# Six places of the instruction order in a decoder-step kernel: where the convolution state is loaded, where squares, one projection step and the last outputs stand, and which order edges there are

## The chip, the cores and the metric

The kernel runs on one core of a Trainium2 chip as one program. The metric is the device time in microseconds (us) of one execution. The five engines appear as PE (TensorE), DVE (VectorE), ACT (ScalarE), POOL (GpSimd) and SP (SyncE, which issues the DMA transfers). Each engine runs its instructions in the order in which the program lists them and waits on semaphores for the others.

## The reference

One layer of a hybrid decoder for 2048 prompt tokens, and for 8 sample sequences of 4 new tokens each. Model width is 1024, the FFN is 2816 wide, all in fp32. Cut to what matters:

```python
def mixer(xn, s0, lp):
    q, k, v, r, a, u, sv = split_cols(xn @ w_in)
    logg = log_sigmoid(a @ w_alpha + b_alpha) / GLA_TAU
    o, S = gla_chunked(q, k, v, logg, s0)          # gated linear attention, with a state
    o = rmsnorm(o, g_gla_out) * silu(r)
    z = sgu_spatial(rmsnorm(gelu(sv), g_sgu), w_s, b_s)
    return concatenate([o, gelu(u) * z], -1) @ w_out, S, sv

def mem_kv(mem, g_mem, wk_x, wv_x):                # 256 memory tokens
    mn = rmsnorm(mem, g_mem)
    return mn @ wk_x, mn @ wv_x

def conv_ffn(hn, buf, w_gate, w_up, conv_w, conv_b, w_down):
    gp = concatenate([buf, hn @ w_gate], axis=1)   # buf: the last two rows (state_conv)
    c = conv_b + sum(conv_w[j] * gp[:, j:j + T] for j in range(3))
    return (gelu(c) * (hn @ w_up)) @ w_down, gp[:, -2:]

h = x + mixer(rmsnorm(x, g_mix), s0, ...)
h = h + mem_attend(rmsnorm(h, g_x), mk, mv, wq_x, wo_x)
h = h + conv_ffn(rmsnorm(h, g_ffn), buf, ...)      # and a final rmsnorm
```

## The kernel before

**Tiling.** The prompt is worked in four sub-blocks of 512 tokens, s = 0 to 3. The 32 sample tokens ride along in the mixer of sub-block 1 (544 columns, as two chunks of 272) and in the FFN of sub-block 2. "Mixer 0" and "mixer 1" are here the mixers of s = 0 and s = 1. Activations lie with the features on the 128 partitions. Every fp32 product is three matmuls of rounded parts (`mm3`, lines 97 to 101): high x high, high x low, low x high. For that, each weight tile is loaded raw (`r_...`, at most 5 in flight), ScalarE writes the rounded part (`h_...`, L84) and VectorE the rest (`l_...`, L85). PSUM has four banks for accumulators (`acc`) and four for everything else (`mps`).

**What sets the order.** The program is a list of `Step`s. `weave(main, (steps, first, last), ...)` spreads side steps over the positions first to last of a main list, and `run` goes through the list and loads weights 5 units ahead. A scheduler of the framework then puts the instructions of each engine in order by a time simulation of its own. `behind(first, then)` adds an edge that only says that `then` comes later in the order than `first`; it makes no semaphore wait between engines.

**Startup.** `mem_load` loads the memory tokens into four buffers `mx`, which the first x tiles `x0` use after them. `mem_norm` transposes them (`mtp`), multiplies by the gain and splits (`mh`, `ml`), and squares them on ScalarE (`junk<-mx`, summed per row in `mss`). The inverse norm is spread to all partitions (`mbc`, copied to `mbcs`). `mem_proj` makes k and v of one head at a time: 48 matmuls `mkp`/`mvp` into two accumulators, which VectorE empties with a multiplication by `mbcs` into `mkf`. `mem_turn` transposes the result for the output (`mkt`, `mvt`), one head later. `late_constants` loads small constants, and the convolution state `state_conv` as six tiles `sc0` to `sc5` with 22 small transposes into one bank `sctp`, copied to `sct`. The FFN of sub-block 2 is the first to read `sct`.

**Mixer 0** also folds weights of the memory attention (`qk_steps`, `vo_steps`): a vo step multiplies two 128-row parts `vr` of v with a weight `wof` (12 matmuls `vop`, two evictions `voh`, `vol`). Of the linear attention, `s0pl` are score matmuls of head pair p and level l, whose inputs `e` and `kr` VectorE and ScalarE make one level after the other. `decay` makes `kh` (VectorE, ScalarE, then POOL), which `keys_turned` transposes (`ktp`). `t_wr` are the gate's projections, `zp` the spatial products, `op` the attention outputs, whose normed and gated form `o` is transposed back as `otp`.

**Output projection.** `out_proj_steps` gives w1, half the sum over the upper inputs (`ch4` to `ch7`, tiles `wo s 4 m`), and w2, the half over the lower ones (`ch0` to `ch3`, from `otp`). Only `whole` sub-blocks (0, 2, 3) keep both halves in one accumulator. In mixer 1 all four w1 steps (`wo140` to `wo143`, 48 matmuls of 272 columns each) stand ahead of the four of w2 (`wo100` to `wo103`), and the edge behind `B.last_o` in `half` does apply to whole sub-blocks only, because it asks for `not end`. After w2 come the memory scores (`sc10...`), which need h of all eight row tiles and sums of them (`wog`, `w1wo`, `wulwo` and others).

**Tail.** `last_rows` makes the last row tiles of y: the product `dr` added to `ht`, squares on ScalarE, a reciprocal root by VectorE and POOL (`rstd_of`, tiles `rt`, `yss`), and the outputs `y`. The outputs of row c follow the norm of row c + 1.

Of the kernel before, what the change touches and what calls it, by code (L numbers as in the profile page):

```python
# [37 lines left out]
def hymba_step_kernel(  # L38
# [48 lines left out]
    def split_scaled(hi, lo, src, g):  # L87
        act.activation(hi, src, AF.Copy, scale=g)
# [223 lines left out]
    def rstd_of(out, ss, p, n, inv):  # L312
        t = narrow("rt")
        dve.tensor_scalar(t[:p, :n], ss, inv, EPS, ALU.mult, ALU.add)
        pool.tensor_tensor(out, t[:p, :n], neghalf[:p, :n], ALU.pow)

# [139 lines left out]


# [76 lines left out]
    def mem_norm():  # L534
        xt, ss = mem_st.xt, narrow("mss")
        mem_st.pair = []
        for k2 in range(4):
            ps = mps(f"mtp{k2}")
            for kk in range(2):
                k = 2 * k2 + kk  # L540
                for c in range(2):
                    pe.transpose(ps[:, kk * 256 + c * 128:kk * 256 + (c + 1) * 128],
                                 xt[c][k // 4][:, (k % 4) * 128:(k % 4 + 1) * 128], ident)
            hi, lo = U(f"mh{k2}", F32R), U(f"ml{k2}", F32R)
            for kk in range(2):
                s = slice(kk * 256, (kk + 1) * 256)
                split_scaled(hi[:, s], lo[:, s], ps[:, s], gcol("gmem", 2 * k2 + kk))
                mem_st.pair.append((hi[:, s], lo[:, s]))
        for c in range(2):
            for j in range(2):  # L550
                act.activation(junk, xt[c][j][:, :512], AF.Square, accum_out=ss[:, 2 * j + c:2 * j + c + 1])
# [9 lines left out]
        act.activation(bc[:, :256], ps[:, :256], AF.Copy)  # L561
# [111 lines left out]
    for nm, w, od in (("k", wk_x, o_mem_k), ("v", wv_x, o_mem_v)):  # L673
        od = od[0, 0].rearrange("m h d -> m (h d)")
        for h in range(4):
            def one(a, b, nm=nm, h=h, od=od):
                mem_proj(nm, h, a, b)
                if mem_st.due:
                    mem_turn(*mem_st.due)
                mem_st.due = nm, h, od  # L680
                if (nm, h) == ("v", 3):
                    mem_turn(*mem_st.due)

            mem_steps.append(Step(one,
                                  [(w[0], 4 * j, 4, h * 256, 256, f"w{nm}{h}{j}") for j in range(2)]))
# [278 lines left out]
    def gla_steps(B):  # L964
# [6 lines left out]
        def gates():  # L971
# [25 lines left out]
            B.P, B.qz, B.kt, B.eb, B.kms, B.b, B.S, B.kh = {}, {}, {}, {}, {}, {}, {}, {}  # L997
# [83 lines left out]
        def keys_turned(p):  # L1081
            kh = B.kh.pop(p)
            ps = mps(f"ktp{s}{p}")
            for c in range(4):
                pe.transpose(ps[:, c * 128:(c + 1) * 128], kh[:, c * 128:(c + 1) * 128], ident)
            t = U(f"kt{s}{p}")
            dve.tensor_copy(t[:, :SB], ps)
            B.kt[p] = t
# [150 lines left out]
    def out_proj_steps(B, unit, src, g, name, sample, first, finished, keep=None, seven=False,  # L1239
# [77 lines left out]
        return ([half(m2, first, False) for m2 in range(4)], [half(m2, second, True) for m2 in range(4)], Step(stat))  # L1317
# [232 lines left out]
    def ffn_steps(B, last=False):  # L1550
# [110 lines left out]
        def last_rows(*ws):  # L1661
# [20 lines left out]
            ready = None  # L1682
            for c in range(4):
# [118 lines left out]
    for s, B in enumerate(blocks):  # L1802
# [72 lines left out]
```

## Time and profile before

| | us |
|---|---|
| median of 3 runs | 2833.33 (2832.15 to 2835.81) |
| the profiled execution | 2834.1 |
| its span in the trace | 2832.4 |
| TensorE busy | 2794.1 |
| VectorE, ScalarE, POOL busy | 1893.4, 1105.7, 572.7 |
| mean granted TensorE clock | 0.995 |

The rows below name engine, line, operation, output <- inputs without buffer numbers, shapes and count. In a row of the waits stand the total, the number and the longest of the waits, behind what ended them. In a timeline row stand start, duration and, in brackets, the idle time ahead with what ended it. A matmul's duration overlaps the next one's; the distance of two starts is what it costs.

### The profile page before, as it was taken

The numbers are of one execution on the slowest core, as the hardware profiler recorded it, in microseconds if no ns is written. First come the engines' busy times: TensorE is split into PE (matmuls) and PEld (weight loads), VectorE is DVE, ScalarE is ACT, GpSimd is POOL, SyncE is SP. The second block draws the span as 40 slices with busy tenths as digits, with TensorE's granted clock in tenths as the row PEclk, the third lists the DMA queues.
The fourth block names the chain that finished last, engine by engine and source line by source line (L and its number), as shares of the span: only waits on it lengthen the run. The fifth ranks groups of instructions, "written<-read, shape, count | busy, mean of one in ns | idle before, by whom it ended". The sixth has DMA issues, their size and how long they took to land.

```text
span 2832.4 us, 47045 instructions
## 1 busy us (share of the span) xinstructions
PE 2794.1 (99%) x17894; PEld 2475.0 (87%) x17894; DVE 1893.4 (67%) x3266; ACT 1105.7 (39%) x1950; POOL 572.7 (20%) x638
## 2 busy tenths in 40 slices
PE   8999999999999999999999999999999999999998
PEld 7887888888887898998888889899999888899997
DVE  6677778777657786655545778666666688665655
ACT  5545445333363444322224445422223545421222
POOL 2001213111101231321311121222221013132222
PEclk9999999999999999999999999999999999999999
DMA  8756479999942246788886315577776324577774
GB/s 290 253 186 223 153 259 340 339 336 331 336 151 62 82 140 218 298 297 289 318 316 208 93 63 198 204 245 258 257 264 218 109 74 137 201 261 276 271 281 175
DMA packets 369687, 638.21 MB, mean 225 GB/s; under 512 B 27370, under 2 KB 238412, under 8 KB 369462
## 3 DMA queue, kind: packets, MB, share of 16 engines
q1 hardware_dynamic: 369462, 635.20, 65.9%
q8 instruction: 142, 2.33, 0.3%
q14 instruction: 83, 0.68, 0.1%
HBM read 507.69 MB, written 127.41 MB: 224 GB/s over the span
## 4 chain that ended last, share of the span: by engine, by line
PE 63%; DVE 3%; DMA 1%; ACT 1%; issue 0%; POOL 0%; POOLq 0%; DVEq 0%; ACTq 0%
PE d L98 4%; PE d L100 4%; PE d L99 4%; PE a_wx L99 2%; PE a_wx L100 2%; PE a_wx L98 2%; PE a_wo L98 1%; PE a_wo L99 1%; PE a_wo L100 1%; PE s L1066 1%; PE a_wu L98 1%; PE a_wu L99 1%; PE t_wr L98 1%; PE a_wu L100 1%; PE t_wr L99 1%; PE t_wr L100 1%
## 5 line engine op out<-in xcount | busy, mean ns | idle before, releaser
L98 PE MATMUL d<-acth,whi_wd 128*128 128x272 f32 (+1 forms) x688 | 235.7, 343 | 1.0 <-DVE h L1724 1.0
L99 PE MATMUL d<-actl,whi_wd 128*128 128x272 f32 (+1 forms) x688 | 233.3, 339 | 0.0
L100 PE MATMUL d<-acth,wlo_wd 128*128 128x272 f32 (+1 forms) x688 | 233.1, 339 | 0.0
L1724 DVE TENSOR_TENSOR h<-d,h 128x512 f32<-128x512 f32 (+1 forms) x232 | 133.5, 581 | 145.1 <-PE d L100 145.1
L1619 POOL TENSOR_TENSOR c<-c,bc_f 128x512 f32<-128x512 f32 (+1 forms) x88 | 136.2, 1552 | 140.4 <-ACT c L1618 139.7
L1609 ACT ACTIVATE c<-g,colsb 128x512 f32<-128x512 f32 x88 | 71.8, 815 | 189.9 <-DVE g L1572 142.9
L100 PEld LDWEIGHTS d<-acth,wlo_wd 128*128 128x128 f32 x688 | 129.2, 188 | 15.7 <-issue 1.2
L98 PEld LDWEIGHTS d<-acth,whi_wd 128*128 128x128 f32 x688 | 129.4, 188 | 14.4 <-DVE h L1724 1.3
L99 PEld LDWEIGHTS d<-actl,whi_wd 128*128 128x128 f32 x688 | 129.6, 188 | 13.6 <-issue 0.4
L1641 POOL TENSOR_TENSOR c<-r_q_wup,c 128x512 f32<-128x512 f32 (+1 forms) x33 | 63.1, 1913 | 330.1 <-DVE r_q_wup L295 209.7
L1606 POOL COPY carry<-g 128x2 f32<-128x2 f32 x88 | 30.9, 351 | 422.8 <-DVE g L1572 391.8
L98 PE MATMUL a_wo<-ch,h_wo 128*128 128x512 f32 (+1 forms) x320 | 111.6, 362 | 2.6 <-ACT r L896 1.4
L99 PE MATMUL a_wo<-cl,h_wo 128*128 128x512 f32 (+1 forms) x320 | 112.7, 356 | 0.8 <-POOL cl L85 0.8
L100 PE MATMUL a_wo<-ch,l_wo 128*128 128x512 f32 (+1 forms) x320 | 111.9, 353 | 0.0
L1610 DVE SCALAR_TENSOR_TENSOR c<-g,colsb,c 128x512 f32<-128x512 f32 x88 | 85.4, 971 | 27.8 <-ACT c L1609 27.3
L100 PE MATMUL a_wx<-pTh,wlo_wx 128*128 128x512 f32 x256 | 101.3, 396 | 0.0
L99 PE MATMUL a_wx<-pTl,whi_wx 128*128 128x512 f32 x256 | 100.8, 394 | 0.0
L98 PE MATMUL a_wx<-pTh,whi_wx 128*128 128x512 f32 x256 | 100.3, 394 | 0.0
L84 ACT ACTIVATE acth<-c 128x512 fp32r<-128x512 f32 (+1 forms) x88 | 55.9, 636 | 113.0 <-DVE c L1641 80.3
L1618 ACT ACTIVATE c<-c 128x512 f32<-128x512 f32 (+1 forms) x88 | 56.1, 638 | 97.1 <-DVE c L1611 85.2
L1611 DVE SCALAR_TENSOR_TENSOR c<-g,colsb,c 128x512 f32<-128x512 f32 x88 | 91.7, 1042 | 1.1
L85 DVE TENSOR_TENSOR actl<-c,acth 128x512 fp32r<-128x512 f32 (+1 forms) x88 | 63.1, 720 | 26.6 <-ACT acth L84 25.7
(3753 smaller groups left out, 9734.4 us busy)
## 6 DMA issues: line engine op xcount, KB each, us to landing
whi_wd<-wd SPq DMA_DIRECT2D x66, 512.0 KB, 9.1
wlo_wd<-wd SPq DMA_DIRECT2D x66, 512.0 KB, 7.4
r_wo<-in_w_out_dram SPq DMA_DIRECT2D x32, 512.0 KB, 3.5
wlo_wx<-vod SPq DMA_DIRECT2D x32, 512.0 KB, 4.6
whi_wx<-vod SPq DMA_DIRECT2D x32, 512.0 KB, 4.8
r_wg<-in_w_gate_dram SPq DMA_DIRECT2D x22, 512.0 KB
r_wup<-in_w_up_dram SPq DMA_DIRECT2D x22, 512.0 KB, 4.8
r_wd<-in_w_down_dram SPq DMA_DIRECT2D x22, 512.0 KB, 4.2
```

Source lines behind the costliest of these rows:

```text
L84: act.activation(hi, src, AF.Copy)
L85: (lo_eng or dve).tensor_tensor(lo, src, hi.bitcast(F32), ALU.subtract)
L98: out = pe.matmul(ps, wh, xh, start=first, stop=False)
L99: pe.matmul(ps, wh, xl, start=False, stop=False)
L100: pe.matmul(ps, wl, xh, start=False, stop=last)
L1609: act.activation(c[:, :SB], g[:, 2:SB + 2], AF.Identity, bias=cb, scale=w2)
L1610: dve.scalar_tensor_tensor(c[:, :SB], g[:, 1:SB + 1], w1, c[:, :SB], ALU.mult, ALU.add)
L1611: dve.scalar_tensor_tensor(c[:, :SB], g[:, 0:SB], w0, c[:, :SB], ALU.mult, ALU.add)
L1618: act.activation(c[:, :T], c[:, :T], AF.Gelu_apprx_tanh)
L1619: pool.tensor_tensor(c[:, :T], c[:, :T], B.fbc[:, :T], ALU.mult)
L1641: (dve, pool)[i].tensor_tensor(c[:, :T], q[i], c[:, :T], ALU.mult)
L1724: dve.tensor_tensor(B.h[m + mm][:, cs], ps[:, :cw], B.h[m + mm][:, cs], ALU.add)
```

## The change

1. `mem_norm`: the four squares get an edge behind the last split (`split_scaled` returns its instruction for that).
2. `mem_turn` goes away: the transposes of a head are written directly behind its projection.
3. The convolution state moves from `late_constants` to a step `sample_conv` at position 9 of mixer 0.
4. `vo_steps` are spread over the positions 11 to 19 instead of 11 to 17, and `keys_turned` goes away: `ktp01` is written directly in `decay`.
5. Edges on w_out: sub-block 0 has none any more; 2 and 3 have one on row tile 2; sub-block 1 gets one, its first w1 matmul behind the last spatial product (`B.last_mix`).
6. In mixer 1 the fourth w1 step (`wo143`) stands ahead of the last w2 step.
7. `last_rows` writes the outputs of a row two norms later instead of one; those of row 1 come behind the last sum `htl`, those of rows 2 and 3 behind the last norm (rows counted from 0).

```diff
@@ mem_norm
-                split_scaled(hi[:, s], lo[:, s], ps[:, s], gcol("gmem", 2 * k2 + kk))
+                last = split_scaled(hi[:, s], lo[:, s], ps[:, s], gcol("gmem", 2 * k2 + kk))
...
-                act.activation(junk, xt[c][j][:, :512], AF.Square, accum_out=ss[:, 2 * j + c:2 * j + c + 1])
+                behind(last, act.activation(junk, xt[c][j][:, :512], AF.Square,
+                                            accum_out=ss[:, 2 * j + c:2 * j + c + 1]))
@@ late_constants
+    def sample_conv():
 
         scd = state_conv[0].rearrange("b t f -> (b t) f")
         sctp = mps("sctp")
...
@@ sgu_steps, mix
-                pe.matmul(ps[:, c * 128:(c + 1) * 128], B.sv[c][:, hs_], wsT[:, h, :], start=True, stop=True)
+                B.last_mix = pe.matmul(ps[:, c * 128:(c + 1) * 128], B.sv[c][:, hs_], wsT[:, h, :], start=True, stop=True)
@@ gla_steps, decay
-            B.kh[p] = kh
-            if s or not p:
-                keys_turned(p)
+            ps = mps(f"ktp{s}{p}")
+            for c in range(4):
+                pe.transpose(ps[:, c * 128:(c + 1) * 128], kh[:, c * 128:(c + 1) * 128], ident)
+            t = U(f"kt{s}{p}")
+            dve.tensor_copy(t[:, :SB], ps)
+            B.kt[p] = t
@@ out_proj_steps
-                            if name == "wo" and not end and (m, k) == (2, 0):
-                                behind(B.last_o, mm)
+                            if name == "wo" and s and not last and k == 0:
+                                if whole and m == 2:
+                                    behind(B.last_o, mm)
+                                elif not whole and m == ci == 0:
+                                    behind(B.last_mix, mm)
...
-        return ([half(m2, first, False) for m2 in range(4)], [half(m2, second, True) for m2 in range(4)], Step(stat))
+        out = [half(m2, second, True) for m2 in range(4)]
+        out.insert(3, half(3, first, False))
+        return [half(m2, first, False) for m2 in range(3)], out, Step(stat)
@@ last_rows
-            ready = None
+            ready = []
...
-                rstd_of(ss[:, 3:4], ss[:, 2:3], 128, 1, 1.0 / D)
-                if ready:
-                    finish(*ready)
-                ready = c, ss
-            finish(*ready)
+                last = rstd_of(ss[:, 3:4], ss[:, 2:3], 128, 1, 1.0 / D)
+                ready.append((c, ss))
+                if c > 1:
+                    finish(*ready.pop(0))
+            cur["added"] = last
+            for one in ready:
+                finish(*one)
@@ the main list
-        folds = [(qk_steps, 0, 10), (vo_steps, 11, 17)] if s == 0 else []
-        steps += weave(proj + w1, *folds, (after, 0, 5), (sgu_st[:1], 6, 6), (sgu_st[1:nst], 11, 11), ...
+        early = [] if s else [Step(sample_conv)]
+        folds = [(qk_steps, 0, 10), (vo_steps, 11, 19)] if s == 0 else []
+        steps += weave(proj + w1, *folds, (after, 0, 5), (sgu_st[:1], 6, 6), (early, 9, 9), (sgu_st[1:nst], 11, 11), ...
```

Where instructions stand now. ScalarE at the startup, before:

```order
L551 ACTIVATE junk_90,mss_287<-mx00_249 128x512
L551 ACTIVATE junk_90,mss_287<-mx01_253 128x512
L88 ACTIVATE mh0_293<-mtp0_288,colsa_247 128x256
L551 ACTIVATE junk_90,mss_287<-mx10_251 128x512
L88 ACTIVATE mh1_304<-mtp1_299,colsa_247 128x256
L551 ACTIVATE junk_90,mss_287<-mx11_255 128x512
L88 ACTIVATE mh0_293<-mtp0_288,colsa_247 128x256
L88 ACTIVATE mh2_315<-mtp2_310,colsa_247 128x256
L84 ACTIVATE h_wk00_259<-r_wk00_257 128x1024
```

ScalarE at the startup, now:

```order
L88 ACTIVATE mh0_293<-mtp0_288,colsa_247 128x256
L88 ACTIVATE mh2_315<-mtp2_310,colsa_247 128x256
L88 ACTIVATE mh1_304<-mtp1_299,colsa_247 128x256
L84 ACTIVATE h_wk00_259<-r_wk00_257 128x1024
L88 ACTIVATE mh3_326<-mtp3_321,colsa_247 128x256
L88 ACTIVATE mh2_315<-mtp2_310,colsa_247 128x256
L84 ACTIVATE h_wk01_265<-r_wk01_263 128x1024
L84 ACTIVATE h_wk10_271<-r_wk10_269 128x1024
L88 ACTIVATE mh3_326<-mtp3_321,colsa_247 128x256
L554 ACTIVATE junk_90,mss_287<-mx00_249 128x512
L84 ACTIVATE h_wk11_277<-r_wk11_275 128x1024
```

The squares moved behind all splits of `mh`; the other three follow between and behind the weight splits, and `mbcs` stands behind `h_wk21`, `h_wk30`, `h_wk31` and the four squares of `x0`, where the three weight splits used to follow it.

TensorE near the end of mixer 0 (the last gate matmuls, the scores of the two upper levels, folds), before:

```order
L98 MATMUL t_wr03_2855<-h_wr03_2864,xh0_7_1211 128x512
L99 MATMUL t_wr03_2855<-l_wr03_2865,xh0_7_1211 128x512
L100 MATMUL t_wr03_2855<-h_wr03_2864,xl0_7_1212 128x512
L1066 MATMUL s015_2914<-kr015_2910,e015_2906 128x2x64 x4
L1066 MATMUL s016_2929<-kr016_2925,e016_2921 128x2x64 x4
L98 MATMUL vop200_2988<-h_wof20_2675,vr20_2984 128x512
```

TensorE at the same place, now:

```order
L99 MATMUL t_wr03_2819<-h_wr03_2828,xh0_7_1175 128x512
L100 MATMUL t_wr03_2819<-l_wr03_2829,xh0_7_1175 128x512
L101 MATMUL t_wr03_2819<-h_wr03_2828,xl0_7_1176 128x512
L1057 MATMUL s015_2882<-kr015_2878,e015_2874 128x2x64 x4
L1057 MATMUL s016_2897<-kr016_2893,e016_2889 128x2x64 x4
L1096 MATMUL ktp01_2916<-ident_81,kh01_2912 128x128 x4
L99 MATMUL vop110_2959<-h_wof11_2643,vr10_2832 128x512
```

`ktp01` follows the scores at once (it came after 56 more fold, spatial and output matmuls). Ahead of these rows, between `zp01` and `s015`, stand 13 gate matmuls, where 22 stood. On VectorE, `l_wof30` and two masked copies now stand between the two inputs of `s016`.

TensorE in mixer 1 (the sample's gate rows `t_wr1q` and `t_wr14`, the spatial products), before:

```order
L732 MATMUL t_wr1q_9622<-r_wr12_9137,sxg_157 32x512 x2
L98 MATMUL a_wo1400_9897<-ch14_9455,h_wo140_9330 128x272
L99 MATMUL a_wo1400_9897<-cl14_9456,h_wo140_9330 128x272
L100 MATMUL a_wo1400_9897<-ch14_9455,l_wo140_9331 128x272
L98 MATMUL a_wo1400_9897<-ch15_9549,h_wo140_9330 128x272
L99 MATMUL a_wo1400_9897<-cl15_9550,h_wo140_9330 128x272
```

TensorE in mixer 1, now:

```order
L723 MATMUL t_wr1q_9622<-r_wr11_9131,sxg_157 32x512 x2
L723 MATMUL t_wr1q_9622<-r_wr10_8920,sxg_157 32x512 x2
L723 MATMUL t_wr1q_9622<-r_wr13_9322,sxg_157 32x512 x2
L723 MATMUL t_wr1q_9622<-r_wr12_9137,sxg_157 32x512 x2
L747 MATMUL t_wr14_9726<-t_wr1t_9691,sum4_151 32x512
L927 MATMUL zp12_9729<-wsT_689,sv10_8297 128x128
```

Before, `t_wr14` and `zp12` came behind 24 matmuls of `wo140`. These left this place; they stand now behind `zp13`, between the state products and the outputs `op`. Further on, the 48 matmuls of `wo143` no longer stand around `otp10<-o13`: `a_wo1000<-ch10` follows that transpose directly.

More of the change, by code (lines that the diff above doesn't have):

```diff
@@ L87, in split_scaled @@
     def split_scaled(hi, lo, src, g):
-        act.activation(hi, src, AF.Copy, scale=g)
+        out = act.activation(hi, src, AF.Copy, scale=g)
         dve.scalar_tensor_tensor(lo, src, g, hi.bitcast(F32), ALU.mult, ALU.subtract)
+        return out
     in_turn = mybir.DependencyInfo(mybir.DependencyClass.NoSync, mybir.DependencyReason.DATA)
@@ L313, in rstd_of @@
         t = narrow("rt")
-        dve.tensor_scalar(t[:p, :n], ss, inv, EPS, ALU.mult, ALU.add)
+        first = dve.tensor_scalar(t[:p, :n], ss, inv, EPS, ALU.mult, ALU.add)
         pool.tensor_tensor(out, t[:p, :n], neghalf[:p, :n], ALU.pow)
+        return first
     def bcast_tokens(rstd, sample, name):
@@ L562, in mem_norm, with mem_proj @@
         mem_st.rs, mem_st.bc = rs, bc
-        mem_st.out, mem_st.t, mem_st.due = {}, {}, None
-    def mem_proj(nm, h, *ws):
+        mem_st.out, mem_st.t = {}, {}
+    def mem_proj(nm, h, od, *ws):
         th, tl, tf = U(f"m{nm}h{h}", F32R), U(f"m{nm}l{h}", F32R), U(f"m{nm}f{h}")
@@ L578, in mem_proj @@
             nc.sync.dma_start(kvd[nm, h][:, x], t[:, :512].bitcast(F32))
-        mem_st.t["f", nm, h] = tf
-    def mem_turn(nm, h, od):
-        tf = mem_st.t.pop(("f", nm, h))
         if h % 2 == 0:
@@ L675, in hymba_step_kernel @@
         for h in range(4):
[L676 to L684, printed above, removed]
+            mem_steps.append(Step(lambda a, b, nm=nm, h=h, od=od: mem_proj(nm, h, od, a, b),
                                   [(w[0], 4 * j, 4, h * 256, 256, f"w{nm}{h}{j}") for j in range(2)]))
@@ L996, in gates @@
             B.lg = lg
-            B.P, B.qz, B.kt, B.eb, B.kms, B.b, B.S, B.kh = {}, {}, {}, {}, {}, {}, {}, {}
+            B.P, B.qz, B.kt, B.eb, B.kms, B.b, B.S = {}, {}, {}, {}, {}, {}, {}
         def cums(p):
@@ L1079, in level @@
                                         ps[:NS, hh * 16:(hh + 1) * 16].rearrange("p (n h) -> p n h", h=half))
[L1081 to L1088, printed above, removed]
         def decay(p):
@@ L1124, in states @@
         def states(p):
-            if p in B.kh:
-                keys_turned(p)
             kv = mps(f"kv{s}{p}")
@@ L1815, in hymba_step_kernel @@
                                       lambda B=B: B.cat, "gx", "wo", B.mix_sample, 4, B.mix_sample, keep, seven=True, whole=not B.mix_sample)
-        folds = [(qk_steps, 0, 10), (vo_steps, 11, 17)] if s == 0 else []
-        steps += weave(proj + w1, *folds, (after, 0, 5), (sgu_st[:1], 6, 6), (sgu_st[1:nst], 11, 11), (sgu_st[nst:nst + 2], 12, 13), (sgu_st[nst + 2:], 16, 16), (gla[:1], 4, 4), (gla[1:2], 6, 6), (gla[2:12], 8, 10), (gla[12:-nlast], 10, 13), (gla[-nlast:], 16, 16), (gtail, 16, 18))
+        early = [] if s else [Step(sample_conv)]
+        folds = [(qk_steps, 0, 10), (vo_steps, 11, 19)] if s == 0 else []
+        steps += weave(proj + w1, *folds, (after, 0, 5), (sgu_st[:1], 6, 6), (early, 9, 9), (sgu_st[1:nst], 11, 11), (sgu_st[nst:nst + 2], 12, 13), (sgu_st[nst + 2:], 16, 16), (gla[:1], 4, 4), (gla[1:2], 6, 6), (gla[2:12], 8, 10), (gla[12:-nlast], 10, 13), (gla[-nlast:], 16, 16), (gtail, 16, 18))
         scales, sc, turns = attention_steps(B)
```

## Prediction

> **What bounds the kernel now.** I read the page first, then the busy time by stretches, then TensorE's waits, and last the timelines of the places that these name.
>
> ```profile
> span 2832.4 us, 47045 instructions
> PE 2794.1 (99%) x17894; PEld 2475.0 (87%) x17894; DVE 1893.4 (67%) x3266; ACT 1105.7 (39%) x1950; POOL 572.7 (20%) x638
> ```
>
> TensorE is the bound: 2794.1 of 2832.4 us. The change leaves its matmuls as many as they are, so it can act only on the 38.3 us in which TensorE stands still, and on matmuls that run at a lower clock after such a stand. The stretches show where both lie (stretch and length, busy time of PE, PEld, DVE, ACT, POOL, granted clock, DMA share, GB/s):
>
> ```profile
> 0.00:12.00 12.00, 4.78 (x18) 3.14 (x18) 3.23 (x11) 6.50 (x15) 10.03 (x47) 1.00 0.72 227
> 12.00:50.00 38.00, 35.90 (x282) 35.17 (x283) 27.98 (x51) 23.96 (x46) 5.96 (x11) 1.00 0.89 289
> 50.00:70.00 20.00, 16.53 (x136) 16.03 (x135) 13.01 (x33) 7.13 (x13) 1.44 (x8) 0.83 0.97 340
> ...
> 245.00:310.00 65.00, 58.63 (x292) 47.73 (x291) 45.44 (x74) 27.25 (x42) 16.06 (x11) 0.92 0.57 185
> ...
> 960.00:1060.00 100.00, 94.80 (x747) 85.95 (x746) 77.35 (x166) 43.65 (x71) 30.81 (x22) 0.98 0.38 124
> ...
> 2820.00:2832.40 12.40, 2.72 (x12) 1.89 (x10) 6.87 (x13) 3.60 (x9) 3.34 (x4) 0.75 0.41 154
> ```
>
> The startup (7.2, 2.1 and 3.5 us idle), the end of mixer 0 (6.4), mixer 1 (5.2) and the tail (9.7) hold 34.1 of the 38.3 us, and the change touches all four. What ended the waits:
>
> ```profile
> PE sctp L466 <- DMA sc<-in_state_conv_dram: 3.1, 1, 3.1
> PE otp L1215 <- DVE o L1209: 3.0, 3, 2.3
> ...
> PE mkp L98 <- ACT h_wk L84: 1.8, 1, 1.8
> PE sc10S L98 <- DVE h L1270: 1.7, 1, 1.7
> PE a_wo L98 <- ACT r L896: 1.4, 1, 1.4
> PE s L1066 <- DVE kr L1056: 1.2, 1, 1.2
> ...
> PE a_wo L99 <- POOL cl L85: 0.8, 1, 0.8
> ```
>
> **1. The convolution state.** Its last transposes wait for a load that SP issued late, and the matmuls behind them run cold:
>
> ```profile
> 52.31 0.63 SPq L463 DMA_DIRECT2D sc<-in_state_conv_dram  x1
> ```
> ```profile
> 60.84 0.39 PE L466 MATMUL sctp<-ident,sc 16*128 16x16 f32 x2 [3.07 <-DMA sc<-in_state_conv_dram]
> ...
> 62.93 0.41 PE L99 MATMUL mvp<-ml,h_wv 128*128 128x256 f32 x1
> 63.14 0.41 PE L100 MATMUL mvp<-mh,l_wv 128*128 128x256 f32 x1
> ...
> 65.74 0.28 PE L98 MATMUL mvp<-mh,h_wv 128*128 128x256 f32 x1
> 65.86 0.28 PE L99 MATMUL mvp<-ml,h_wv 128*128 128x256 f32 x1
> ```
>
> Behind the gap matmuls start 0.21 us apart, later 0.12. Some 12 of them lose 0.09 each, and the transposes beside them a little: 1.2 us. The 22 transposes and their copy cost the same in mixer 0, where TensorE is busy throughout. The six loads go into SP's queue there between fold stores and weights; at 0.63 us each or less they delay the `vr` and `wof` loads behind them by a few us, which are issued many units ahead. Gain 3.07 + 1.2 = 4.3 (bounds 3.1, the idle alone, and 5.0).
>
> Whether a gap costs clock decides here and below. [...]
>
> **2. Squares behind the splits.** ScalarE no longer runs squares ahead of the first weight split, but what needs the squares comes later:
>
> ```profile
> 8.49 0.62 ACT L551 ACTIVATE junk<-mx 128x512 bf16<-128x512 f32 x1
> 9.01 0.19 ACT L551 ACTIVATION_READ_ACCUMULATOR junk<-mx 128x1 f32 x1
> ...
> 10.79 1.06 ACT L84 ACTIVATE h_wk<-r_wk 128x1024 fp32r<-128x1024 f32 x1
> ...
> 20.61 0.37 ACT L561 ACTIVATE mbcs<-mbc 128x256 f32<-128x256 f32 x1
> ```
> ```profile
> 27.98 0.33 PE L589 MATMUL mkt<-ident,mkf 128*128 128x128 f32 x1 [1.02 <-DVE mkf L575]
> ```
>
> Two squares of 0.8 stand directly ahead of `h_wk`; without them it starts near 9.5 and the first `mkp` 1.3 earlier (the 1.8 row shrinks to 0.5). The price: `mbcs` scales every projection, so no accumulator is emptied before it. In the new order the four memory squares follow most of the splits, the loads of x reuse their buffers and so wait for them, and three more weight splits stand ahead of `mbcs`: 20.6 + 4 x 0.8 + 3 x 1.06 = 27.0. TensorE, two heads (96 matmuls) on and with four accumulators full, stood at this `mkt` from 26.9 on before; 1.3 earlier, and without the four transposes of x that lay ahead (0.6), it comes at about 25.0 and stands until `mkt` gets its input near 27.8: 2.8 new, with 1.1 of cold matmuls behind it. Gone are the 2.1 idle of 12 to 50, this `mkt` among them, which hang on the same chain. Net -1.3 + 2.8 + 1.1 - 2.1 = +0.5. Bounds: -2.5 if `mbcs` comes in time, +3.5 if the x loads make it three us later.
>
> The transposes of k and v that lose their hand-made delay stand one step behind their projection in the order all the same: nothing.
>
> **3. Mixer 0: later folds, `ktp01` at once.** TensorE had 22 matmuls between `zp01` and `s015`; now it has 13; 9 at 0.23 are 2.1 us less. VectorE's chain between them stays: z, e, a split of w_out, e again, kr.
>
> ```profile
> 251.15 0.74 DVE L939 SCALAR_TENSOR_TENSOR z<-zp,colsb,bsb 128x512 f32<-128x512 f32 x1
> ...
> 256.09 0.87 DVE L1056 SCALAR_TENSOR_TENSOR kr<-e,sel,q 128x256 f32<-128x256 f32 x2
> ```
> ```profile
> 259.41 2.05 PE L1066 MATMUL s<-kr,e 128*128 128x128 f32 x8 [1.17 <-ACT h_wof L84]
> ```
> ```profile
> 260.45 1.21 DVE L85 TENSOR_TENSOR l_wof<-r_wof,h_wof 128x1024 fp32r<-128x1024 f32 x1
> ```
> ```profile
> 260.60 2.20 POOL L1111 TENSOR_TENSOR kh<-kh,k 128x512 f32<-128x512 f32 x1 [4.71 <-ACT kh L1110]
> ```
> ```profile
> 298.00:308.00 10.00, 9.86 (x33) 7.58 (x33) 2.73 (x4) 2.24 (x4) 0.00 (x0) 0.72 0.01 2
> ```
>
> So `s015` waits 1.2 + 2.1 = 3.3. `s016` has a fold split like the one shown (1.2) and two masked copies newly inside its chain: 2.6 instead of 1.2. `ktp01` follows at once and needs kh, which POOL ended at 262.8, 3.4 after `s016` began; less the 1.1 of `s016` at full clock it waits 2.3. That is 8.2 instead of 2.4: +5.8. Most is given back: VectorE, which sets the waits at `otp` (3.0, and a clock of 0.72 in the 10 us behind them, 0.28 x 10 less what was idle: 2.3), and POOL's `cl` (0.8) have then had 6 us to catch up, and 12 fold matmuls stand directly ahead of `otp`. I take back 4.8 of these 6.1: net +1 (bounds -4, if VectorE is earlier than I count; +6, if `otp` waits as before).
>
> **4. The edges on w_out in mixer 1 (sub-block 1).** Until now 24 matmuls of w_out covered the copy that `t_wr14` needs:
>
> ```profile
> 964.99 1.92 PE L732 MATMUL t_wr1q<-r_wr,sxg 128*32 128x512 f32 x16
> ```
> ```profile
> 969.91 0.62 ACT L736 ACTIVATE t_wr1t<-t_wr1q 128x512 f32<-128x512 f32 x1
> ```
>
> Now `t_wr14` follows `t_wr1q` directly: idle from 966.91 to about 970.6, 3.7 instead of 1.4, and above the 3.07 that went cold: +2.3 + 1.2 = +3.5 (bounds +1, +4.5). ScalarE is late through a weight load and a table load, which stay. The edges of sub-blocks 2 and 3 leave the order as it was: nothing.
>
> **5. The moved step.** The fourth step over the upper half, 48 matmuls of about 0.125 (6.0 us), stood between the transposes `otp10` and the next projection; now it stands ahead of the last step.
>
> ```profile
> 1003.60 0.69 ACT L88 ACTIVATE ch<-otp,colsb 128x512 fp32r<-128x512 f32 x1 [1.54 <-PE otp L1215]
> ```
> ```profile
> 1030.00:1050.00 20.00, 16.24 (x112) 15.07 (x111) 17.52 (x33) 13.03 (x23) 9.46 (x5) 0.91 0.18 54
> ```
>
> Without that cover `a_wo1000` waits for `ch10` (0.3 + 0.7 behind `otp10`), and `otps10` for the gate, 0.4: +1.4 (bounds 0.5, 2.5). In return VectorE, nearly full in 1030 to 1050, gets the 6 us exactly ahead of the score matmuls, whose waits make the 3.76 us of idle there and cost 1.0 of clock: -4.8 at best; I take -4.6 (bounds -1, -4.8). Its weight load (512 KB) is issued three units later, while the DMA share is low. Net -3.2.
>
> **6. Tail.** The third row's norm now goes ahead of the outputs of the second:
>
> ```profile
> 2821.98 2.41 DVE L1676 SCALAR_TENSOR_TENSOR y<-ht,yss,gf 128x512 f32<-128x512 f32 x2
> ...
> 2828.10 0.75 DVE L1676 SCALAR_TENSOR_TENSOR y<-htl,yss,gf 128x512 f32<-128x512 f32 x1 [0.66 <-POOL yss L315]
> ```
> ```profile
> 2822.09 0.40 PE L99 MATMUL dr<-wlo_wd,acth 128*128 128x512 f32 x1
> 2822.32 0.40 PE L100 MATMUL dr<-whi_wd,actl 128*128 128x512 f32 x1
> ```
>
> `htl` goes right behind the last matmul (2822.8; before, the two outputs ended only at 2824.4), its square and the last reciprocal run beside the y outputs, and the 0.66 wait for POOL vanishes. (The two matmuls also show the 0.23 used above.) The last y comes at about 2826.6: -1.5 (bounds -1.0, -1.8; the last stores then follow at their old distance).
>
> **Sum**: -4.3 + 0.5 + 1 + 3.5 - 3.2 - 1.5 = -4.0. The profiled execution took 2834.1 us (span 2832.4 and 1.7 around it), so 2830.1; the median of the runs, 2833.33, is 0.8 lower, so 2829.3. A measurement of this kernel tells about 0.2%, 5.7 us, from no change.
>
> **Rivals.**
> - *Mixer 0 gains.* VectorE reaches `kr015` before TensorE does, since two evictions and a split of the folds now come later, and the 6.4 us idle of 245 to 310 and the clock lost there (0.08 of 65 us) go for the most part, 8 of 11. For it: VectorE is idle for 30% of that stretch. Against: z needs `zp01`, and the chain behind it is fixed. Then -4.0 - 1 - 8 = -13, with half of it -9: 2820 to 2825.
> - *Slower.* The place is `s015`, `s016`, `ktp01`. If nothing of the 5.8 comes back, because the `otp` waits hang on VectorE alone (two more evictions of folds stand ahead of its last gate), and the new gap costs a clock like the one behind `otp` (2.3), mixer 0 costs 8 to 10: the sum is +3 to +5, 2836 to 2838. It decides from 5 us in mixer 0 on.
> - *The moved step does nothing*: the score waits hang on the last output step, which still comes directly ahead of them. Then -4.0 + 3.6 = -0.4: 2833.
>
> **How the numbers follow.** Forecast (-1.5 to -6.5) 0.46; mixer 0 gains 0.27; moved step idle 0.15; slower 0.12. Faster by over 0.2% are nearly all of the second case and the end of the first (0.14): 0.40. Slower by over 0.2% is the far end of the last, and a sum of upper bounds: 0.07. The rest, 0.53, is within 0.2%. The range runs from the middle of the gain case, 2821.5, into the slow one, 2835.5; the forecast's own is 2826.5 to 2831.5.
>
> **What would show it.** In the new profile: no wait at `sctp` and full clock in 50 to 70; `mkp` starting near 10.6 and a wait at `mkt` near 25 to 28; waits at `s015`, `s016` and `ktp01` of 3.3, 2.6 and 2.3 and one below 1.5 at `otp`; a 3.7 us wait of `t_wr14`; two small ones near `otp10`; none at the scores; the last y 1.5 earlier from the end of the matmuls. Wrong it would be above all by mixer 0, whose chain I moved by hand, and by `mbcs`.

## The result and the profile after

The changed kernel takes 2838.66 us (median of 14 runs, 2835.53 to 2843.09), the kernel before 2833.35 in the same group of runs. The ratio is 1.0020, 95% interval 1.0012 to 1.0029: about 5 us slower. The prediction said 2829.3 with a range of 2821.5 to 2835.5. In what follows a ratio is always to the kernel before, run on the same chip in turn; 0.0010 is 2.8 us. One execution of the kernel before took 5555 us and is left out of the ratio.

The page's first lines of the changed kernel, profiled once:

```profile
span 2837.0 us, 47062 instructions
...
PE 2799.4 (99%) x17894; PEld 2479.6 (87%) x17894; DVE 1892.2 (67%) x3266; ACT 1107.4 (39%) x1950; POOL 567.4 (20%) x638
```

The matmuls are as many as before, and TensorE's idle time is too: 2837.0 - 2799.4 = 37.6 us, 38.3 before. What grew is the busy time, by 5.3 us. The same matmuls took longer, so the place to read next is the granted clock. The stretches (length, busy time of PE, PEld, DVE, ACT, POOL, clock, DMA share, GB/s):

```profile
0.00:12.00 12.00, 5.59 (x21) 4.10 (x21) 3.94 (x9) 5.70 (x10) 9.08 (x45) 1.00 0.77 239
12.00:50.00 38.00, 36.53 (x293) 36.28 (x293) 29.77 (x58) 26.98 (x54) 5.42 (x12) 1.00 1.00 328
50.00:70.00 20.00, 18.83 (x163) 18.43 (x161) 14.72 (x38) 8.78 (x15) 1.05 (x1) 1.00 0.94 315
245.00:310.00 65.00, 55.98 (x269) 45.86 (x269) 45.35 (x70) 28.08 (x44) 15.84 (x11) 0.87 0.58 194
960.00:1060.00 100.00, 93.50 (x700) 84.09 (x698) 74.01 (x158) 42.02 (x68) 28.08 (x22) 0.93 0.32 103
2820.00:2837.00 17.00, 9.12 (x45) 7.16 (x43) 10.34 (x22) 7.77 (x19) 3.87 (x5) 0.88 0.37 139
```

The stretch 50 to 70 is at full clock (0.83 before). The end of mixer 0 fell from 0.92 to 0.87 and mixer 1 from 0.98 to 0.93. (The trace's record of the clock begins at 16.8 us here and at 16.9 in the kernel before, so the 1.00 of the first rows says nothing of the time ahead of it: in both kernels the first `mkp` matmuls start 0.21 us apart, and 0.12 from 16.9 us on.) The record of both kernels shows two values, 1.0 and 0.5, so the time at half clock is 2 x (1 - clock) x length: 17 us of 65 and 14 us of 100, where the record has 10 and 3.4 before. Half of what TensorE is busy in these stretches is lost (the `vop` matmuls of 128x512 start 0.43 us apart up to 265.7 us and 0.23 from 266.1 us on, where the longest of them ends); what it stands idle in them is counted among the waits already. This longest one has 3.6 us of idle:

```profile
252.35:266.00 13.65, 10.02 (x32) 8.42 (x33) 9.60 (x18) 2.47 (x5) 1.72 (x1) 0.50 0.27 91
```

Counted so, the clock cost mixer 0 6.6 us where it had cost 4.8, and mixer 1 6.8 where it had cost 1.6. The waits changed places (us in total, number, longest):

```profile
PE s L1057 <- DVE kr L1047: 5.0, 2, 3.3
PE t_wr L747 <- ACT t_wr1t L727: 3.6, 1, 3.6
...
PE otp L1198 <- DVE vol L85: 2.2, 2, 1.3
PE a_wo L99 <- ACT ch L88: 2.1, 4, 0.8
PE mkp L99 <- ACT h_wk L84: 2.1, 1, 2.1
...
PE mkt L588 <- DVE mkf L579: 1.4, 1, 1.4
...
PE t_ws L99 <- ACT xh L88: 1.2, 1, 1.2
PE a_wk L99 <- ACT sv L880: 1.2, 1, 1.2
PE ktp L1096 <- POOL kh L1093: 0.9, 1, 0.9
```

Gone are `sctp` (3.1) and most of the score waits `sc10` (3.8 then, 0.9 now). New are 5.0 at `s015` and `s016`, 0.9 at `ktp01`, 3.6 at `t_wr14`, and two of 1.2 earlier in mixer 0 (`t_ws` at 70 us, `a_wk` at 107).

To place gains and losses I cut the span at five rows of TensorE's timeline; these are the changed kernel's:

```profile
68.32 0.28 PE L101 MATMUL mvp<-mh,l_wv 128*128 128x256 f32 x1
...
335.23 0.28 PE L99 MATMUL sc00A<-whi_qk00A,w1wo 128*128 128x256 f32 x1
...
966.43 1.93 PE L723 MATMUL t_wr1q<-r_wr,sxg 128*32 128x512 f32 x16
...
1069.69 0.28 PE L99 MATMUL sc11A<-whi_qk11A,w1wo 128*128 128x256 f32 x1
...
2828.72 0.40 PE L101 MATMUL dr<-whi_wd,actl 128*128 128x512 f32 x1
```

"Startup" ends with the last `mvp`, "mixer 0" with the start of the first `sc00A`, "mixer 1" runs from the end of `t_wr1q` to the start of the first `sc11A`, "tail" from the end of the last `dr` to the end of the span. The transposes of the convolution state, 1.55 us, merely changed from the startup to mixer 0:

```profile
174.31 1.55 PE L469 MATMUL sctp<-ident,sc 16*128 16x16 f32 x22
```

| stage | before | after | difference | predicted |
|---|---|---|---|---|
| startup | 76.9 | 68.6 | -8.3 (-6.8 without the transposes) | -3.8 |
| mixer 0 | 257.3 | 266.6 | +9.3 (+7.8) | +1 |
| up to the sample's gate rows | 632.7 | 633.1 | +0.4 | 0 |
| mixer 1 | 96.3 | 101.3 | +5.0 | +0.3 |
| up to the last `dr` | 1759.5 | 1759.4 | -0.1 | 0 |
| tail | 9.7 | 7.9 | -1.8 | -1.5 |

So the two mixers lost 12.8 us where 1.3 were forecast, and the startup gained 3 us more than forecast. In mixer 1 the clock alone, 5.2 us more, is as much as the whole difference; mixer 0 stood idle 5.2 us longer and lost 1.8 more to the clock. This is one profile of each kernel; the experiments repeat these stages.

### The profile page after: what moved, and what is told of

It reads as the page before. It is cut to its first block, busy times and chain, and to the rows that moved or that the text cites. A ratio compares the mean times of both kernels' runs of the same rounds, so it can differ in the third digit from the quotient of the medians.

```text
span 2837.0 us, 47062 instructions
## 1 busy us (share of the span) xinstructions
PE 2799.4 (99%) x17894; PEld 2479.6 (87%) x17894; DVE 1892.2 (67%) x3266; ACT 1107.4 (39%) x1950; POOL 567.4 (20%) x638
## 4 chain that ended last, share of the span: by engine, by line
PE 63%; DVE 3%; ACT 1%; DMA 0%; issue 0%; POOL 0%; DVEq 0%; ACTq 0%
PE d L101 4%; PE d L100 4%; PE d L99 4%; PE a_wx L101 2%; PE a_wx L100 2%; PE a_wx L99 2%; PE s L1057 1%; PE a_wo L99 1%; PE a_wo L100 1%; PE a_wo L101 1%; PE a_wu L99 1%; PE a_wu L100 1%; PE t_wr L99 1%; PE a_wu L101 1%; PE t_wr L100 1%; PE t_wr L101 1%
## 5 line engine op out<-in xcount | busy, mean ns | idle before, releaser
L100 PEld LDWEIGHTS d<-actl,whi_wd 128*128 128x128 f32 x688 | 129.4, 188 | 13.7 <-issue 0.4
```

What stands on the lines that cost most here:

```text
L100: pe.matmul(ps, wh, xl, start=False, stop=False)
```

## The experiments

Theory 1: what counts is where TensorE loses its cover, and each such gap costs its idle time and a stretch at half clock behind it. Its rivals are that only the idle time counts, that the gap comes back elsewhere, and, for mixer 0, the prediction's own cause (later folds and the undelayed `ktp01`).

**e1, the changed kernel again**, as the base of its group.

> The changed kernel as it is, beside the others of this group. Both theories: 1.001 to 1.003 of the kernel before (2837 to 2842 us); in the profile 13 to 14 us at half clock around s015 to vop11, and two stretches of 7 us behind t_wr14 and behind otp10. If these stretches lie elsewhere or are shorter in a second profile, the clock is no property of the order and theory 1 (the loss is matmuls at half clock behind new gaps) is weak.

Ratio 1.0016 (1.0007 to 1.0025), median 2838.0. The waits in the mixers are the same to 0.5 us, and the half clock isn't: behind `t_wr14` and behind `otp10` there were 3.4 us of it instead of 6.8, around `s015` 10.2 instead of 13.7, and 3.4 us came in the startup, where the first profile has none. Shorter stretches were named as a sign against theory 1, and they did come.

More profiles show how far it goes. TensorE's order of instructions is the same in the changed kernel, e1, e2, e3 and e6 up to mixer 1. All five have a half-clock stretch around `s015` (10.2 or 13.7 us, with 6 us of waits) and one at `otp` (3.4 or 6.8, with 3 us of waits); only e2 and e6 have 3.4 us more near 109 us, behind the wait of 1.2 at `a_wk` that all five have and another of 1.3 or 0.4, and 3.4 us near 181. So at the large waits the stretch came in every execution, at small ones in some, and its length changed from one execution to the next.

**e4, the convolution state three positions later:**

```diff
-        steps += weave(proj + w1, ..., (early, 9, 9), (sgu_st[1:nst], 11, 11), ...
+        steps += weave(proj + w1, ..., (early, 12, 12), (sgu_st[1:nst], 11, 11), ...
```

> The changed kernel with the convolution state's transposes at position 12 of mixer 0 instead of 9, nothing else. In the order of instructions 34 gate and fold matmuls then stand between zp01 and s015, where 13 stood (22 in the kernel before). Theory 1 with this cause (the transposes stand among the scores of the first pair at position 9 and push the score chain of the second behind the gate's matmuls): the waits of 5.0 us at s015 and s016 and 0.9 at ktp01 go, with most of the 13.7 us at half clock (6.8 us lost): 7 to 11 us faster, 2828 to 2832. Rival (the later folds and the undelayed ktp01 uncover the scores, as the prediction had it): these stay as they are, so at most 2 us, 2837 to 2839.

Ratio 0.9991 (0.9982 to 1.0000), median 2831.7: 6.3 us less than e1 by the medians, 7 by the ratios, at the lower end of what theory 1 expected. The waits at `s015` and `s016` are gone but for 0.3 (1.8 at `ktp01` is left), and so is the half clock in 250 to 275. First the changed kernel's row of that stretch, then e4's:

```profile
250.00:275.00 25.00, 19.03 (x81) 16.09 (x81) 18.03 (x27) 11.96 (x19) 4.71 (x4) 0.73 0.49 162
```
```profile
250.00:275.00 25.00, 22.84 (x133) 19.13 (x132) 20.94 (x33) 13.78 (x21) 7.66 (x6) 1.00 0.71 236
```

One number moved the loss of mixer 0. The edges, the folds and `ktp01` stayed as they were in the change. The stages of several profiles agree: mixer 0 took 266.6 to 270.4 us in the five with the state at 9 named above, and 260.3 to 262.0 in the three with it at 12 and the same order up to mixer 1 (e4, e5, e10), 7.0 us less in the mean.

**e8 and e9, the move alone, in the kernel before**: the 22 transposes taken out of `late_constants` into `sample_conv`, once at position 9, once at 13.

```diff
+    def sample_conv():
+
         scd = state_conv[0].rearrange("b t f -> (b t) f")
...
+        early = [] if s else [Step(sample_conv)]
-        steps += weave(proj + w1, *folds, ..., (sgu_st[1:nst], 11, 11), ...
+        steps += weave(proj + w1, *folds, ..., (early, 9, 9), (sgu_st[1:nst], 11, 11), ...
```

> The kernel before with nothing changed but the place of the convolution state (position 9 of mixer 0). The prediction's step 1: 4.3 us faster, 2829.3, mixer 0 as before. Theory 1: the startup gains its 4 to 5 us, and mixer 0 gives them back, since 13 instead of 22 gate matmuls stand ahead of s015: 2.1 us more wait there at least, and up to 5 with a longer half-clock stretch: 2831 to 2835. By stages: startup about 69 to 72 instead of 76.9, mixer 0 262 to 267 instead of 257.3, of which some 2.5 are the transposes themselves.

> The kernel before with the convolution state at position 13 of mixer 0 instead of the startup, nothing else. Its order keeps 22 gate matmuls between zp01 and s015, as in the kernel before (e8, with the state at position 9, has 13 and gained nothing). Theory 1 (the place among the scores spoils the move, the move itself is good): the startup's gain of 5 to 7 us (some 1.5 of it transposes that only move) is kept, s015 waits 1.2 to 1.6 as before: 2827 to 2830, 0.998 to 0.999. Rival (whatever is gained at the startup is lost at the next wait, since VectorE and ScalarE set mixer 0): 2832 to 2834, as e8.

At position 9 the ratio is 1.0006 (0.9997 to 1.0015), median 2834.3: no gain. At 13 it is 0.9981 (0.9972 to 0.9990): 5.4 us faster. Both are what theory 1 expected. The startup gained the same in both (69.7 and 70.3 us, 76.9 before); mixer 0, 257.3 before, took 264.3 with the state at 9 and 258.2 at 13, the 1.55 of the transposes in both. Of the rest in e8, 3.3 us are the two score waits (5.7 against 2.4) and 1.3 three small new waits; the time at half clock stayed 10.2 us. TensorE at the upper scores, at 9 and then at 13:

```profile
255.95 1.13 PE L1068 MATMUL s<-kr,e 128*128 128x128 f32 x8 [3.28 <-DVE kr L1058]
259.47 2.05 PE L1068 MATMUL s<-kr,e 128*128 128x128 f32 x8 [2.40 <-DVE kr L1058]
```
```profile
253.70 2.04 PE L1068 MATMUL s<-kr,e 128*128 128x128 f32 x8 [2.04 <-DVE kr L1058]
```

3.28 and 2.40 are close to the 3.3 and 2.6 that the prediction worked out for `s015` and `s016`, in a kernel that has neither the later folds nor the undelayed `ktp01`. Counted in the instruction order, 22 gate matmuls (`t_wr`) stand between `zp01` and `s015` in the kernel before and in e9, 13 in e8 and in the changed kernel, 34 in e4. At position 9 `sctp` comes between `s001` and `s002`, and the scores of both pairs come later: `s002` behind 28 matmuls of `a_wu` instead of none, `s014` behind 83 gate matmuls instead of 74. The gate's matmuls are a fixed number, so fewer are left for `s015`. Why the scheduler holds the scores back there (the six `sc` tiles come from the same pool as `e` and `kr`) is read from the code and was not tried.

**e7, folds at 11 to 17 and `ktp01` delayed as before**, the state still at 9:

```diff
-        folds = [(qk_steps, 0, 10), (vo_steps, 11, 19)] if s == 0 else []
+        folds = [(qk_steps, 0, 10), (vo_steps, 11, 17)] if s == 0 else []
...
-            ps = mps(f"ktp{s}{p}")
...
+            B.kh[p] = kh
+            if s or not p:
+                keys_turned(p)
```

> The changed kernel with the folds at 11 to 17 again and ktp01 delayed again, the convolution state still at position 9. Theory 1 (the convolution state is what uncovers s015): still 13 gate matmuls between zp01 and s015, so its waits of 3.3 and 1.7 us and most of the half clock stay; only the 0.9 of ktp01 goes: 2836 to 2838. The prediction's step 3 (later folds and ktp01 cost it): the 5.9 us of waits there and about 5 us for the clock shrink to the 2.4 and 1.7 of before: 2830 to 2833.

Both missed: 1.0043 (1.0031 to 1.0056), median of 5 runs 2844.6, 6 to 8 us slower than the changed kernel. The waits at `s015` and `s016` stayed (3.3 and 1.7), so folds and `ktp01` are not their cause. But taking them back put a new wait at the attention outputs:

```profile
297.94 0.44 PE L1206 MATMUL otp<-ident,o 128*128 128x128 f32 x2 [0.33 <-DVE o L1200]
305.49 3.07 PE L1206 MATMUL otp<-ident,o 128*128 128x128 f32 x12 [6.29 <-DVE o L1200]
```

Mixer 0 took 274.0 us, 6.0 more than the mean of the five profiles above. Among the other parts of the change, this one gains 6 to 8 us; the prediction had charged it with a loss.

**e2 and e3, the edge on sub-block 1.** e2 removes it; e3 keeps it and fills the wait with matmuls that are thrown away (the real product overwrites them; two more edges hold them and `zp12` in place):

```diff
-                                elif not whole and m == ci == 0:
-                                    behind(B.last_mix, mm)
```
```diff
                 ps[4] = mps(f"t_{name}4")
+                if name == "wr1":
+                    for i in range(14):
+                        behind(ps["s"], pe.matmul(ps[4], xs[0][0][:, :128], wh[:, i % 2], start=True, stop=True))
```

> The changed kernel without the edge of sub-block 1: 24 matmuls of w_out stand again between t_wr1q and t_wr14. Theory 1 (a gap costs its idle time and then a stretch at half clock): the wait of 3.6 us shrinks to about 1.4 and the 6.8 us at half clock behind it go, 2.1 + 3.4 = 5.5 us, so about 2833, 1.000 of before. Theory 2 (only the idle time counts, the half clock would come anyway a little later): 2.1 us, 2836.5. Theory 3 (the 24 matmuls are missing at their later place, so the gap reappears there): no change, 2838.7.

> The changed kernel with 14 idle-time matmuls (128x512, about 0.23 us each, 3.2 us in all) written into the accumulator of t_wr14 directly ahead of it; the real product overwrites them. They do no work that is used and can't make t_wr14 earlier: its input comes at the same moment. Theory 1: the clock stays at 1.00 behind t_wr14, 6.8 us at half clock less, so 3.4 us faster: about 2835.3, though nothing is waited for less. Theory 2 (the idle time itself is the loss): 2838.7, or up to 1 us slower where the 14 end after the input is there.

Ratios 1.0013 (1.0004 to 1.0022) and 1.0008 (0.9999 to 1.0017). Against e1 that is 1 and 2 us less, each uncertain by 3.6, so the totals decide neither; the 1.000 that theory 1 gave for e2 lies outside its interval. The stage does better, since it leaves out what the other stages happened to do: mixer 1 took 101.3, 98.6, 101.3 and 98.4 us in the four profiles with edge and moved step (the changed kernel, e1, e4, e7), 98.9 in e6 with the edge and the step in its old place, 96.9 in e2 and 97.2 in e3. TensorE in e3 at that place, and the stretch in e1 and in e3:

```profile
970.08 3.53 PE L751 MATMUL t_wr<-h_wr,xh 128*128 128x512 f32 x14
973.54 1.04 PE L752 MATMUL t_wr<-t_wr1t,sum 128*32 128x512 f32 x2
```
```profile
960.00:985.00 25.00, 21.16 (x114) 15.54 (x113) 17.63 (x35) 10.85 (x17) 5.78 (x5) 0.93 0.44 148
```
```profile
960.00:985.00 25.00, 25.00 (x165) 19.50 (x164) 15.62 (x34) 10.27 (x15) 8.89 (x8) 1.00 0.38 128
```

The 14 matmuls do nothing useful and release nothing sooner, yet the stage is 2.7 us shorter than the mean of the four, 99.9. The clock's record says why: behind `t_wr14` it has 6.8, 3.4, 6.8 and 6.8 us at half clock in the four, which lost 1.7 to 3.4 us, and none in e3. So most of the 2.7 is the price of the clock (the waits at `otp10` are 0.3 us shorter in e3, too), as far as one profile of e3 can tell. It is nearly all that removing the edge saves (3.0 by the same mean, not the 5.5 that theory 1 expected: a wait of 1.5 us comes back in front of the 24 matmuls).

**e5, e4 and e2 together** (state at 12, no edge).

> Both changes of e2 and e4 together: the transposes of the convolution state at position 12, and no edge on sub-block 1. From the stages of e2 (mixer 1 from the sample's gate rows to the second score group: 96.9 us, where the changed kernel took 101.3 and 98.6 and e4 took 101.3) theory 1 expects 2 to 4.5 us less than e4: 2827 to 2830, 0.9975 to 0.999 of before. Theory 3 (the edge is worth nothing, as the medians of e2 say): 2831.7 again.

Ratio 0.9978 (0.9968 to 0.9987), median 2826.8: 6 us faster than the kernel before. It is 3.7 us less than e4, as expected, but uncertain by 3.7 too: the total agrees with the stages (96.4 against 101.3) and doesn't prove the edge's cost by itself.

**e6 and e10, the moved step taken back**, in the changed kernel and in e5:

```diff
-        out = [half(m2, second, True) for m2 in range(4)]
-        out.insert(3, half(3, first, False))
-        return [half(m2, first, False) for m2 in range(3)], out, Step(stat)
+        return ([half(m2, first, False) for m2 in range(4)], [half(m2, second, True) for m2 in range(4)], Step(stat))
```

> The changed kernel with all four upper output steps of mixer 1 ahead of the lower ones again, as before. Theory 1: the waits of 0.8 and 0.8 us at otps10 and a_wo1000 and the half clock around 1010 to 1017 (3.4 to 6.8 us of it, 1.7 to 3.4 lost) go, 3.3 to 5.0 us; the score waits come back (3.8 us in the kernel before, and 1.7 for a half-clock stretch of 3.4, against 0.9 now), 4.6 us: 2837.5 to 2839.5, no change. The prediction's step 5 (the move gains 3.2): 2841 to 2842. [...]

> The kernel of e5 with the four upper output steps of mixer 1 ahead of the lower ones again. Here t_wr14 is covered, so the moved step is seen by itself: waits of 0.8 and 0.8 us and 6.8 at half clock around otp10 go, score waits of 2.8 against 1.4 us and 3.4 at half clock come. Theory 1: 0 to 2 us slower than e5, 2826.8 to 2829. The prediction's step 5 (3.2 us): 2830.

Ratios 1.0023 (1.0013 to 1.0032) and 0.9991 (0.9982 to 1.0000): 2 and 3.7 us slower than e1 and e5, each uncertain by 3.7. Both point to a gain by the move, and e10's median, 2829.9, is the 2830 of the prediction's step 5. The stage doesn't confirm it: without the edge, mixer 1 took 96.9, 96.4, 97.0 and 97.4 us with the step moved (e2, e5, e11, e12) and 96.3, 97.1, 98.0 and 95.6 with it in the old place (before, e8, e9, e10), means of 96.9 and 96.7. TensorE in e5, with the step moved, and in e10, without:

```profile
998.76 0.39 PE L99 MATMUL a_wo<-ch,h_wo 128*128 128x272 f32 x1 [0.78 <-ACT ch L88]
999.98 0.60 PE L100 MATMUL a_wo<-cl,h_wo 128*128 128x272 f32 x1 [0.83 <-DVE cl L89]
1033.34 0.39 PE L99 MATMUL a_wo<-ch,h_wo 128*128 128x272 f32 x1 [0.42 <-DVE h L1254]
1039.87 0.39 PE L101 MATMUL sc10A<-whi_qk10A,w1wo 128*128 128x256 f32 x1 [0.41 <-DVE w1wo L85]
1044.14 0.39 PE L101 MATMUL sc10S<-h_qk10S,wtlwo 128*128 128x256 f32 x1 [0.56 <-DVE wtlwo L85]
```
```profile
1034.62 0.39 PE L99 MATMUL sc10S<-h_qk10S,wthwo 128*128 128x256 f32 x1 [1.69 <-DVE h L1254]
...
1041.52 0.39 PE L99 MATMUL sc10A<-whi_qk10A,wbhwo 128*128 128x256 f32 x1 [0.83 <-ACT wbhwo L84]
```

And e5's stretch around the first of these waits:

```profile
985.00:1025.00 40.00, 38.40 (x281) 36.00 (x279) 31.96 (x69) 15.20 (x26) 10.03 (x8) 0.91 0.35 106
```

The score waits do shrink (4.5 us in e10's six rows, 1.4 in e5's three), but 1.6 us of waits come at `otp10`, and 7 us at half clock with them. Between 0 and 4 us of gain the runs leave this open.

**e11 and e12**, two more parts taken back in e5: `ktp01` delayed as in e7, and the edge of the squares removed.

```diff
-                behind(last, act.activation(junk, xt[c][j][:, :512], AF.Square,
-                                            accum_out=ss[:, 2 * j + c:2 * j + c + 1]))
+                act.activation(junk, xt[c][j][:, :512], AF.Square, accum_out=ss[:, 2 * j + c:2 * j + c + 1])
```

> The kernel of e5 with ktp01 delayed again behind the folds, the folds still at 11 to 19. The wait of 1.8 us at ktp01 goes; but the states and outputs op that need it come 21 matmuls later, and with them o and its gates on VectorE. If that is what made e7 slower (its otp waited 6.3 us once, against 2.6 in all now): 3 to 6 us slower than e5, 2830 to 2833. If e7 was slower by the folds alone: 1 to 2 us faster, 2825.

> The kernel of e5 without the edge that puts the four squares of the memory behind the splits. By stages the startup took 69.7 us with the old squares (e8) and 68.5 to 70.4 with the new ones (one run 72.4), so theory 1 expects no change: 2825.5 to 2828. The prediction's step 2 (the edge costs 0.5, between -2.5 and +3.5): 2826.3, the same. Rival (the wait of 1.4 to 3.4 us at mkt, and the half clock that follows it in one profile, comes from the late mbcs and is a loss): 2823 to 2825.

e11: 0.9994 (0.9985 to 1.0002), median 2829.3, 2.5 us slower than e5 by the medians, 4.5 by the ratios (uncertain by 3.6), though its one profile has a shorter span (2825.7 against 2826.7) and a shorter mixer 0 (259.4 against 260.8). Its waits at `otp` are 5.4 us against 2.6 in e5, as the chain through the outputs would have it, and the 1.8 at `ktp01` is gone; what that costs in all is open. e12: 0.9971 (0.9962 to 0.9981), median 2824.9, the fastest of all and within the rival's 2823 to 2825; but its 2 us against e5 are uncertain by 3.7. Its mixer 0 is 4.4 us shorter than e5's, and 3.3 of that is the clock (3.4 us at half clock against 10.2). So whether the edge of the squares costs anything stays open.

No run takes back the transposes of k and v (part 2) or the edges of sub-blocks 0, 2 and 3 by themselves.

## Why the prediction was wrong

1. **The convolution state** was the step that failed. The gain at the startup came, and larger: with this step alone, and without the 1.55 of the transposes, the startup is 5.7 (e8) and 5.1 us (e9) shorter, against 4.3. (Part of that: the half clock behind the gap lasted until 64.7 us and cost 1.9, where the working counted 1.2.) But the working said that the 22 transposes "cost the same in mixer 0, where TensorE is busy throughout". Their own 1.55 us do; their place doesn't. They push the scores behind, and in e8 mixer 0 lost 264.3 - 257.3 - 1.55 = 5.5 us by it. Alone, the step gains nothing (e8, +1.7 us with an interval that holds zero) instead of 4.3; at another position it gains 5.4 (e9). In the changed kernel, position 12 instead of 9 makes mixer 0 7.0 us shorter in the mean.
2. **Squares**: forecast +0.5. `mkp` came 1.0 earlier, but its wait, which was to shrink from 1.8 to 0.5, grew to 2.1, because TensorE got there earlier as well. And since the first matmuls start 0.21 us apart up to 16.9 us in both kernels, the earlier start put TensorE only 5 matmuls ahead there, 0.6 us. `mkt` waits 1.4 us, in e1 3.4, where 2.8 was worked out. The runs don't tell 0.5 from nothing.
3. **Mixer 0**: the waits were nearly sized right (3.3, 1.7 and 0.9 against 3.3, 2.6 and 2.3), with the wrong cause: the count of 13 instead of 22 was put down to the folds, because they stand there, and it came from the convolution state. Two terms were mis-sized. The give-back of 4.8 at `otp` and `cl` was 0.7: `otp`, `ch` and `cl` waits of 3.7 us before are 3.05 now, because VectorE's fold evictions `vol`, which the later folds bring there, replace the gates. And the clock behind the new gap, to which the sum gave nothing: 17.1 us at half clock in 245 to 310 instead of 10.2, which, less the idle in them, lost 6.6 us instead of 4.8. (Behind `otp` the clock had cost 3.2 before, not the 2.3 of the working.) The scores and `ktp01` (6.0 instead of 2.4, +3.6), -0.7, the clock (+1.8) and the two unforeseen waits of 1.2 make 7.1, where the stage shows 7.8. The first of these two, at `t_ws`, takes back a part of the startup's gain: TensorE arrives earlier, its next input doesn't (in e12 the wait is missing, and `t_ws` starts at 70.2 us, in the changed kernel at 70.0). The cause of the second is open. The rival "slower" named this place and 2836 to 2838; I had left it 0.12. Its 8 to 10 us for mixer 0 were 7.8. That its total came within 1 us is luck: the startup and mixer 1, which it left as forecast, were off by -3.0 and +4.7.
4. **The edge**: forecast +3.5, a wait of 3.7. It waits 3.6 us (1.4 before), and by the stages it costs 3.0; the totals of e4 and e5 say 3.7, uncertain by as much. The mechanism was right, and so was the size as far as these runs tell; the clock, put at 1.2, cost 1.7 or 3.4 in the five profiles that have this wait.
5. **The moved step**: forecast -3.2. The score waits mostly went, as forecast (3.8 us to 0.9), and the waits at `otp10` came as forecast (1.55 against 1.4). Overlooked was the clock there: 6.8 us at half clock in that profile, 3.4 lost, which can take the whole gain. How much of it is left, the runs leave open.
6. **Tail**: forecast -1.5, measured -1.8: 7.9 us in all eleven profiles that have it, 9.7 in the three that don't.

Steps 1 to 3 together, forecast at -2.8, came to +1.0 (startup and mixer 0). Steps 4 and 5, forecast at +0.3, came to +5.0 in the profile shown and to +3.2 by the means (99.9 against 96.7).

## What to carry to other kernels

The 1.55 us of transposes, moved onto a busy TensorE, made mixer 0 0.9 us longer at position 13 (e9) and 7.0 us at position 9 (e8), where the scheduler put the scores behind more of the gate's matmuls. So after each part of a change, alone, count the independent matmuls that stand between a chain's start and its consumer, at the places that had little to spare. Here that count (13, 22, 34) told e8, e9 and e4 apart before they ran. And price a gap on TensorE at its idle time plus what the clock loses, here in steps of about 1.7 us, half of a piece of 3.41 us at half clock. In these profiles the single wait of 3.5 to 3.8 us at `t_wr14` lost one or two steps each time; two waits of 0.8 us among small transposes (`otp10`) lost two in six of eight profiles, one in one and none in one; the single waits of 1.2 to 1.5 us ahead of `wo140` lost none in eight. Where a gap can't be covered by work, matmuls that are thrown away may do as cover: in e3's one profile they left no half clock behind `t_wr14` and a stage of 97.2 us against a mean of 99.9.

## What was not expected of the hardware

The half clock came in pieces of 3.41 us and multiples of it: by the trace's record of the granted clock, which begins at some 15 to 18 us, 6.83, 3.41, 6.83 and 3.41 us in the kernel before, 13.65, 3.41, 6.83 and 6.83 in the changed one, and 3.4, 6.8, 10.2 or 13.7 us at every place of all these kernels but the tail. The same wait cost a different number of pieces from one execution to the next: `t_wr14` waited 3.6, 3.8, 3.5, 3.7 and 3.7 us (after, e1, e4, e6, e7), and 6.8, 3.4, 6.8, 3.4 and 6.8 us at half clock came with it. In e5, waits of 0.3 and 1.8 us at `s015` and `ktp01` brought 3.4 us of it, and in e12 the same waits none; in e10, 4.5 us of waits in six parts at the scores brought none. What sets how many pieces a wait brings, these runs don't show. For a reader of profiles this means that one profile of a kernel can be 3 us off in one stage through the clock alone (mixer 1 took 101.3 us in the changed kernel's first profile, with 13.7 us at half clock, and 98.6 in e1's, with 6.8), and that stages of several profiles, or medians of ten runs, are needed to tell a part of this size.

The fastest version tried is e12, 0.9971 (0.9962 to 0.9981) of the kernel before: the change with the convolution state at position 12 and without the edges of sub-block 1 and of the squares.
